# A two-layer hybrid decoder on one core: the list scheduler's durations for the matmul engine are rewritten

## The chip, the cores and the metric

The kernel runs on one NeuronCore of one Trainium2 chip. The metric is the device time of one execution in microseconds (us); lower is better. Shown are the median of three runs, and one execution that the hardware profiler recorded.

## What is computed

Two decoder layers, for a prompt of 512 tokens and for 8 sequences of 8 new tokens (64 more), 576 tokens in all. Each layer projects the normalised input, runs a chunked retention and a sparse attention (an indexer picks the 128 or 66 best keys), gates both, merges them and projects again. All inputs and outputs are fp32. Cut down:

```python
def decoder_layer(x, p_i, pos, ret_s0, past, topk, ...):
    h = rmsnorm(x, g_norm)
    rq, rk, rv, rz, aq, ak, av, az, iq, ik, iw, gr, ga = in_projection(h, w_in, pos, q_gain, k_gain)
    o_r, s_new = retention(rq, rk, rv, ret_s0)
    u_r = (group_norm_heads(o_r) * silu(rz)) @ w_o_ret
    o_a = sparse_attention(aq, pos, k_all, v_all, iq, iw, ik_all, topk)
    u_a = (o_a * silu(az)) @ w_o_att
    m = sigmoid(gr) * u_r + sigmoid(ga) * u_a
    x = x + m @ w_out
    x = x + sigmoid(x @ w_ple_gate) * (p_i @ w_ple_proj)
    return x, ak, av, ik, s_new
```

## The kernel before

**The work.** Every projection is computed in fp32r from two parts: a weight tile of 128x1024 fp32 is loaded by SyncE (SP), rounded by ScalarE (ACT) into `whi`, and the remainder goes to `wlo` by VectorE (DVE) (`convert`, line 440). The moving data are split the same way (`xh`, `xl`). Each block of 128 channels then takes three matmuls: high by high, low by high, high by low. `proj_a` (line 457) makes a 128-channel unit of 48 such matmuls over two halves of 288 tokens, so 288 columns each; the token-major projections take 256, 260 or 320 columns. They write three PSUM banks called `pm`, which DVE and ACT empty.

**The order.** The kernel is written as many sequential generators ("streams"): the main stream, which walks through PLAN (projections, merge, output, gating), and side streams: statistics, tables, the indexer, attention heads (`head`, line 898, three in flight), the sample's attention, retention, and one for each weight load and each bank to be emptied. A stream yields one instruction at a time. `Streams.go` (line 277) is a list scheduler that runs while the program is built: it keeps a clock for each engine, asks for each waiting instruction when its inputs would be ready (`_ready`, line 251), picks the one that could start first (on a tie the lower priority number, then the older stream), emits it, and moves the engine's clock by `op.dur`. On the chip each engine executes its own instructions in the order emitted, and semaphores hold an instruction until its inputs are there. So the durations do not change any instruction; they decide the order on all five queues: PE, DVE, ACT, POOL and SP.

**The table of durations** is `_duration` (line 142). For PE it gives a transpose 0.110 us; a matmul in fp32r `max(n, 64) / 2400 + 0.003` us for n columns; one in plain fp32 `4 * max(n, 64) / 2400` us, times 0.55 when the stationary tile has at most 64 columns, and a small figure when it has at most 32. For DVE it gives (n + 64) / 960 us and for ACT (n + 112) / 1200 us (61 in place of 112 out of PSUM), with additions for scalar pointers. To the end of a producer `_ready` adds a hand-over time (`HOP`, line 199: 0.23 us from ACT to PE, 0.21 from DVE to PE), and for a DVE or ACT instruction fed by another engine a margin of 0.15 or 0.1 us (`MARGIN`, line 103).

**Places that matter below.** An attention head multiplies queries with keys into bank `tq` (two fp32r matmuls), takes the softmax on DVE and ACT (tile `t2k`, row sums in `sm`), transposes the result on PE into bank `ta`, copies it out by ACT, and multiplies with the values into bank `oT`. That last step is in plain fp32 with a stationary tile of 64 columns, one matmul for each block of 128 keys, which the trace shows as two passes. Before the merge the main stream waits for all side streams (line 1254, `for e in sides`), after which the gated results are split into `oh` and `ol`. The only arithmetic on POOL is the power -0.5 in `rsqrt`.

Of the kernel before, what the change touches and what calls it, by code (L numbers as in the profile page):

```python
# [16 lines left out]
OP = mybir.AluOpType  # L17
# [86 lines left out]


class Op:
    __slots__ = ("eng", "fn", "a", "k", "name", "outs", "ins", "dur")

    def __init__(self, eng, fn, name, a, k):
        self.eng, self.fn, self.name, self.a, self.k = eng, fn, name, a, k  # L110
        aps = [x for x in list(a) + list(k.values()) if isinstance(x, bass.AP)]
        out = k.get("out", a[0] if a else None)
        acc = k.get("accum_out")
        self.outs = [_box(x) for x in (out, acc) if x is not None]
        self.ins = [_box(x) for x in aps if x is not out and x is not acc]
        self.dur = _duration(eng, name, out, aps, a, k)


def _val(x):
    return x() if callable(x) else x  # L120


def _box(ap):
    span = 1 + sum(s * (n - 1) for s, n in list(ap.ap)[1:])
    t = ap.tensor
    if ap.space in (bass.MemoryType.SB, PSUM):
        row = list(ap.ap)[0][0] or 1
        p0 = _val(ap.start_partition)
        c0 = ap.offset % row if row > 1 else 0
        return t.name, p0, p0 + _val(ap.partition_size), c0, c0 + span  # L130
    first = list(ap.ap)[0]
    return t.name, 0, 1, ap.offset, ap.offset + span + first[0] * (first[1] - 1)


def _free(ap):
    n = 1
    for s, c in list(ap.ap)[1:]:
        n *= c
    return n


def _duration(eng, name, out, aps, a, k):
    n = max(_free(x) for x in aps)
    psum = any(x.space == PSUM for x in aps[1:])
    if eng == "PE":
        if name == "transpose":
            return 0.110
        lhs = aps[1]
        if lhs.dtype == FT:
            if _free(lhs) <= 32:  # L150
                return 0.030 + n * 0.4e-3
            return 4 * max(n, 64) / 2.4e3 * (0.55 if _free(lhs) <= 64 else 1.0)
        return max(n, 64) / 2.4e3 + 0.003
    if eng == "DVE":
        if name == "memset":
            return (n + 8) / 0.96e3
        ptr = sum(1 for x in aps[1:] if _free(x) == 1 and n > 4 and x.space != PSUM)
        if name in ("tensor_scalar", "tensor_copy") and not psum and all(x.dtype == FT for x in aps[:2]):
            return (n / 2 + 66) / 0.96e3 + 0.062 * min(ptr, 2)
        return (n + 64) / 0.96e3 + 0.062 * min(ptr, 2)  # L160
    if eng == "ACT":
        ptr = sum(1 for x in aps[1:] if _free(x) == 1 and n > 1)
        return (n + (61 if psum else 112)) / 1.2e3 + 0.093 * min(ptr, 2)
    if eng == "POOL":
        return 0.3 + 0.165 * n
    return {"page": 0.5, "gather": 0.74}.get(name, 0.47)


# [24 lines left out]


class Streams:
    """Emits the instructions of many sequential streams in the order in which a model of the engines could
    start them, so that each engine's program order follows what is ready."""

    HOP = {("DVE", "DVE"): 0.13, ("ACT", "ACT"): 0.13, ("POOL", "POOL"): 0.1, ("PE", "PE"): 0.0, ("SP", "SP"): 0.0,
           ("ACT", "PE"): 0.23, ("DVE", "PE"): 0.21, ("PE", "DVE"): 0.2, ("PE", "ACT"): 0.2, ("POOL", "DVE"): 0.07,  # L200
# [2 lines left out]
    def __init__(self):  # L203
        self.clock = dict.fromkeys(("PE", "DVE", "ACT", "POOL", "SP"), 0.0)
        self.dma = 0.0
        self.log = {}
        self.heads = []
        self.run = []
        self.count = 0

    def spawn(self, gen, prio):
        self.count += 1
        self.run.append(([gen, prio, self.count, None, 0.0], None))
# [63 lines left out]
    def go(self):  # L277
        clock = self.clock
        while True:
            while self.run:  # L280
                st, value = self.run.pop(0)
                self._advance(st, value)
            if not self.heads:
                return
            best = None
            for i, st in enumerate(self.heads):
                key = (max(clock[st[3].eng], st[4]), st[1], st[2])
                if best is None or key < best[0]:
                    best = (key, i)
            st = self.heads.pop(best[1])  # L290
            op = st[3]
            start = best[0][0]
            op.fn(*op.a, **op.k)  # L293
            end = start + op.dur
            clock[op.eng] = end
            if op.eng == "SP" and op.name != "page":
                size = _val((op.a[0] if op.a else op.k["out"]).nbytes)
                self.dma = max(self.dma, start + 1.1) + size / 0.35e6
                end = self.dma + 1.0
            self._note(op, end)  # L300
            self._advance(st, None)
# [3 lines left out]
def tile_hybrid_decoder(ctx: ExitStack, tc: tile.TileContext, A, O):  # L305
# [3 lines left out]
    V, S, PE, SP, G = (Engine(n, o) for n, o in (("DVE", nc.vector), ("ACT", nc.scalar), ("PE", nc.tensor),  # L309
                                                 ("SP", nc.sync), ("POOL", nc.gpsimd)))  # L310
# [78 lines left out]
    ready, paged = Event(), Event()  # L389
    second, third = Event(), Event()  # L390

    # ---- weights: one ordered sequence of units, each split into two float32r parts as it lands
    W = {}

    class Unit:
# [1155 lines left out]
```

## Time and profile before

| | |
|---|---|
| three runs | 1131.04, 1131.97, 1132.43 us; median 1131.97 |
| span of the profiled execution | 1130.3 us, 21562 instructions (its own time is not given apart from the span) |
| PE (matmuls) | 1116.5 us busy, 99%, 8586 instructions |
| weight loads of PE | 1058.9 us, 94% |
| DVE / ACT / POOL | 725.6 / 512.5 / 45.7 us busy (64%, 45%, 4%) |
| DMA | 105.92 MB, mean 94 GB/s |

Matmuls overlap in the records: a matmul of 288 columns is shown as 0.30 us long, but the next one starts 0.13 us after it. What PE spends on an instruction is therefore read from start to start in the timeline, not from the duration of one.

### The profile page before, as it was taken

What the parts mean: (1) busy time and instruction counts of PE and PEld (TensorE: products, weight loads), DVE (VectorE), ACT (ScalarE), POOL (GpSimd) and SP (SyncE); (2) the same over time, 40 slices, a digit from 0 to 9 for tenths busy, and PEclk for the clock granted to TensorE, in tenths of its full rate; (3) what the DMA queues carried; (4) which work ended last, traced back from release to release, by engine and by line L of the source; (5) the groups of instructions that cost most, each with busy time, mean ns of one, the idle gap of its engine ahead of it and who ended that gap; (6) DMA issues with size and microseconds to landing.
All of it is one profiled execution on the core that took longest, in us unless ns stands there. A gap on an engine that the chain in (4) does not pass through costs nothing.

```text
span 1130.3 us, 21562 instructions
## 1 busy us (share of the span) xinstructions
PE 1116.5 (99%) x8586; PEld 1058.9 (94%) x8586; DVE 725.6 (64%) x1883; ACT 512.5 (45%) x1084; POOL 45.7 (4%) x52
## 2 busy tenths in 40 slices
PE   8999999999999999999999999999999999999998
PEld 7899988888899999999999999888889999999998
DVE  6799988876464444543658999888654553544343
ACT  6643566647443232324546336656563422222331
POOL 0100200000000000000010012000000000000000
PEclk9999999999999999999999999999999999999999
DMA  6442221322122222523336112222212222234231
GB/s 196 139 133 76 76 75 52 102 78 78 59 75 75 93 76 92 172 92 109 100 118 181 59 57 94 74 79 80 73 60 78 75 78 91 75 130 144 93 113 48
DMA packets 43895, 105.92 MB, mean 94 GB/s; under 512 B 6418, under 2 KB 18578, under 8 KB 43794
## 3 DMA queue, kind: packets, MB, share of 16 engines
q1 hardware_dynamic: 43794, 104.55, 27.4%
q8 instruction: 67, 1.10, 0.4%
q14 instruction: 34, 0.28, 0.1%
HBM read 93.61 MB, written 10.91 MB: 92 GB/s over the span
## 4 chain that ended last, share of the span: by engine, by line
PE 91%; DVE 4%; DMA 2%; ACT 2%; issue 1%; SPq 0%; POOL 0%; DVEq 0%; ACTq 0%; POOLq 0%
PE pm L293 72%; PE oT L293 5%; PE tq L293 4%; PE acc L293 3%; PE tr L293 3%; PE ta L293 3%; DVE wlo L293 1%; DMA wst<-in_wb 1%; ACT whi L293 1%; DVE misc L293 1%; DMA x<-in_xT 1%; DVE silz L293 0%; DMA wst<-in_wq 0%; DVE qs L293 0%; DVE ol L293 0%
## 5 line engine op out<-in xcount | busy, mean ns | idle before, releaser
L293 PE MATMUL pm<-xl,whi 128*128 128x288 f32 x1536 | 458.7, 299 | 0.0
L293 PE MATMUL pm<-xh,wlo 128*128 128x288 f32 x1536 | 458.4, 298 | 0.0
L293 PE MATMUL pm<-xh,whi 128*128 128x288 f32 x1536 | 458.0, 298 | 0.4 <-DVE misc L293 0.4
L293 PEld LDWEIGHTS pm<-xl,whi 128*128 128x128 f32 x1536 | 290.1, 189 | 3.2 <-issue 2.4
L293 PEld LDWEIGHTS pm<-xh,whi 128*128 128x128 f32 x1536 | 290.2, 189 | 2.9 <-issue 1.6
L293 PEld LDWEIGHTS pm<-xh,wlo 128*128 128x128 f32 x1536 | 289.9, 189 | 1.8 <-issue 1.4
L293 ACT ACTIVATE whi<-wst 128x1024 fp32r<-128x1024 f32 (+4 forms) x148 | 150.5, 1019 | 280.5 <-PE pm L293 207.7
L293 DVE TENSOR_TENSOR wlo<-wst,whi 128x1024 fp32r<-128x1024 f32 (+4 forms) x148 | 173.0, 1171 | 88.8 <-ACT whi L293 88.5
L293 PE MATMUL pm<-whi,xh 128*128 128x256 f32 (+2 forms) x416 | 117.2, 288 | 0.7 <-ACT xl L293 0.7
L293 PE MATMUL pm<-wlo,xh 128*128 128x256 f32 (+2 forms) x416 | 117.0, 289 | 0.0
L293 PE MATMUL pm<-whi,xl 128*128 128x256 f32 (+2 forms) x320 | 91.0, 284 | 0.0
L293 DVE TENSOR_TENSOR misc<-pm,R 128x288 f32<-128x288 f32 x64 | 29.2, 457 | 90.1 <-PE pm L293 88.7
L293 ACT ACTIVATE t2k<-t2k,sm 128x256 f32<-128x256 f32 (+3 forms) x136 | 75.6, 581 | 22.6 <-DVE sm L293 19.4
L293 PEld LDWEIGHTS pm<-whi,xh 128*128 128x128 f32 x416 | 78.7, 189 | 2.5 <-issue 1.2
L293 PEld LDWEIGHTS pm<-wlo,xh 128*128 128x128 f32 x416 | 78.7, 189 | 1.6 <-issue 1.1
L293 PE MATMUL pm<-oh,whi 128*128 128x288 f32 x240 | 71.0, 296 | 0.0
L293 PE MATMUL pm<-oh,wlo 128*128 128x288 f32 x240 | 70.9, 296 | 0.0
L293 PE MATMUL pm<-ol,whi 128*128 128x288 f32 x240 | 70.9, 295 | 0.0
L293 PEld LDWEIGHTS pm<-whi,xl 128*128 128x128 f32 x320 | 60.5, 189 | 0.1
L293 ACT ACTIVATE misc<-misc 128x288 f32<-128x288 f32 x64 | 27.9, 436 | 60.5 <-DVE misc L293 60.5
L293 DVE MAX8 sm<-xl 128x8 f32<-128x384 f32 (+2 forms) x96 | 52.3, 548 | 0.3
L293 DVE SCALAR_TENSOR_TENSOR misc<-misc,pm 128x288 f32<-128x288 f32 x60 | 26.8, 451 | 39.3 <-PE pm L293 39.3
(231 smaller groups left out, 1654.3 us busy)
## 6 DMA issues: line engine op xcount, KB each, us to landing
wst<-in_wa SPq DMA_DIRECT2D x96, 512.0 KB, 3.5
wst<-in_wb SPq DMA_DIRECT2D x16, 512.0 KB, 4.1
wst<-in_wo SPq DMA_DIRECT2D x16, 512.0 KB, 3.4
s<-in_ckv SPq DMA_DIRECT2D x32, 128.0 KB, 2.4
s<-in_s SPq DMA_DIRECT2D x8, 512.0 KB, 4.3
out_rss<-s SPq DMA_DIRECT2D x8, 512.0 KB, 2.6
x<-in_xT SPq DMA_DIRECT2D x8, 288.0 KB, 4.5
misc<-in_xT SPq DMA_DIRECT2D x8, 288.0 KB, 3.6
```

The lines of the kernel that those rows point to most:

```text
L293: op.fn(*op.a, **op.k)
```

## The change

It edits the scheduler's model of the matmul engine. The entries for fp32r and for plain fp32 matmuls get other formulas; each PE instruction carries its array form (whether the stationary tile has more than 64 rows, and whether it has up to 32, up to 64 or more columns), and when the form differs from that of the PE instruction emitted before, 0.09 us is added to PE's clock after the instruction has been chosen. The POOL entry keeps its figure for powers and gets a smaller one for other operations. Two comments become blank lines. No instruction is added or removed.

```diff
@@ class Op
-    __slots__ = ("eng", "fn", "a", "k", "name", "outs", "ins", "dur")
+    __slots__ = ("eng", "fn", "a", "k", "name", "outs", "ins", "dur", "form")
...
+        self.form = (_val(a[1].partition_size) > 64, min(2, _free(a[1]) - 1 >> 5)) if eng == "PE" else None
@@ def _duration
             if _free(lhs) <= 32:
                 return 0.030 + n * 0.4e-3
-            return 4 * max(n, 64) / 2.4e3 * (0.55 if _free(lhs) <= 64 else 1.0)
-        return max(n, 64) / 2.4e3 + 0.003
+            return 2 * max(0.11, n / 1.2e3 + 0.005)
+        return max(0.108, (n + 32) / 2.4e3)
...
     if eng == "POOL":
-        return 0.3 + 0.165 * n
+        return 0.3 + (0.165 if k.get("op", a[-1]) == OP.pow else 0.0022) * n
@@ class Streams
+        self.form = None
...
             op.fn(*op.a, **op.k)
+            if op.form != self.form and op.eng == "PE":
+                start += 0.09
+                self.form = op.form
             end = start + op.dur
             clock[op.eng] = end
```

## Rows read from the trace of the kernel before

**Rows 1.** The page: engines over the span, the granted clock in 40 slices.
```profile
PE 1116.5 (99%) x8586; PEld 1058.9 (94%) x8586; DVE 725.6 (64%) x1883; ACT 512.5 (45%) x1084; POOL 45.7 (4%) x52
...
PEclk9999999999999999999999999999999999999999
```

**Rows 2.** The chain that ended last, in order of time: start us, us, what.
```profile
315.99 9.71 PE pm L293 x73
326.09 1.42 DVE ol L293 x2
...
332.68 235.60 PE pm L293 x1776
```

**Rows 3.** By stretch: us, PE, PEld, DVE, ACT, POOL busy, PEclk, DMA share, GB/s.
```profile
60.00:140.00 80.00, 79.64 (x613) 75.44 (x612) 75.95 (x232) 34.69 (x76) 9.45 (x9) 1.00 0.26 89
140.00:240.00 100.00, 99.79 (x787) 87.12 (x785) 84.97 (x275) 61.59 (x160) 4.91 (x6) 1.00 0.24 82
```

**Rows 4.** PE's waits over the whole span: us in total, times, longest.
```profile
PE oT L293 <- ACT whi L293: 5.2, 1, 5.2
PE oT L293 <- DVE ol L293: 0.8, 2, 0.4
```

**Rows 5.** Timeline of PE, matmuls of 256 columns, 120.0 to 121.5 us.
```profile
120.02 0.28 PE L293 MATMUL pm<-whi,xl 128*128 128x256 f32 x1
...
121.43 0.28 PE L293 MATMUL pm<-whi,xl 128*128 128x256 f32 x1
```

**Rows 6.** Timeline around a change of array form, 711.2 to 712.1 us.
```profile
711.20 0.29 PE L293 MATMUL pm<-xl,whi 128*128 128x288 f32 x1
...
711.42 0.43 PE L293 MATMUL oT<-t2k,xl 128*64 128x128 f32 x2
...
711.79 0.40 PE L293 MATMUL pm<-xh,wlo 128*128 128x288 f32 x1
...
712.03 0.30 PE L293 MATMUL pm<-xh,whi 128*128 128x288 f32 x1
```

**Rows 7.** Timeline of PE through two attention heads, 285.0 to 288.6 us.
```profile
285.03 1.09 PE L293 MATMUL oT<-t2k,xl 128*64 128x128 f32 x8
286.05 0.66 PE L293 MATMUL ta<-cst,t2k 128*128 128x128 f32 x4
286.46 0.48 PE L293 MATMUL tq<-kdh,qs 128*128 128x512 f32 x1
...
287.01 0.29 PE L293 MATMUL pm<-xl,whi 128*128 128x288 f32 x1
...
288.29 0.54 PE L293 MATMUL oT<-t2k,xl 128*64 128x128 f32 x3
```

**Rows 8.** Groups of PE instructions over the span, shapes kept apart: the product with the values.
```profile
L293 PE MATMUL oT<-t2k,xl 128*64 128x128 f32 x320 | 48.7, 283 | 0.0
```

**Rows 9.** Timeline of all engines around a wait of PE, 49.0 to 49.6 us.
```profile
49.08 0.39 ACT L293 ACTIVATE t2k<-tq 128x256 f32<-128x256 f32 x1
49.53 0.19 PEld L293 LDWEIGHTS tq<-kdh,iqs 128*128 128x128 f32 x1 [0.88 <-ACT t2k L293]
```

**Rows 10.** Timeline of DVE in the crowded stretch, 90 to 96 us.
```profile
90.20 1.22 DVE L293 TENSOR_TENSOR wlo<-wst,whi 128x1024 fp32r<-128x1024 f32 x1
91.34 0.45 DVE L293 SCALAR_TENSOR_TENSOR silz<-tb,silz 128x288 f32<-128x288 f32 x1
91.72 0.07 DVE L293 MATCH_VALUE_LOAD sc<-sm,sc 64x8 f32 x1
```

**Rows 11.** Waits of PE's weight loads in 40 to 326 us: total, times, longest.
```profile
PEld tq L293 <- ACT t2k L293: 0.9, 1, 0.9
PEld ta L293 <- ACT t2k L293: 0.8, 2, 0.4
PEld ta L293 <- DVE misc L293: 0.7, 2, 0.5
PEld ta L293 <- DVE qs L293: 0.5, 2, 0.3
```

## The prediction

> **What bounds the kernel now.** I read the page first. PE is busy for 1116.5 of 1130.3 us and its granted clock is full, 2.4 GHz, in all 40 slices [rows 1]. The chain in order of time comes second: half of each layer is one unbroken run of PE, such as 1776 matmuls in 235.60 us [rows 2]. The views by stretch and of the waits come third: in the attention part DVE is busy for 75.95 of 80 us (95%), later for 85 of 100 [rows 3], and PE hardly waits. Its largest wait, 5.2 us, is for the first weights, and 0.8 us is lost at the two merges [rows 4]. In the first layer's attention part the larger waits of its weight loads come to 2.9 us [rows 11]. So the bound is PE's own work, the same 8586 instructions in any order. An order can change two things only: how often PE waits, and how often it changes its array form.
>
> **What the table says and what the trace says.** Times are from start to start.
> - A matmul of 288 columns took 235.60 / 1776 = 0.1327 us [rows 2]. The old entry is 0.123 (8% short), the new one 0.133.
> - One of 256 columns took (121.43 - 120.02) / 12 = 0.1175 us [rows 5]; old 0.110, new 0.120.
> - The product with the values: 1.02 us for four of them and the change of form behind them, less 0.09 us, makes 0.23 us each [rows 7]; old 4 x 128 / 2400 x 0.55 = 0.117, new 0.223.
> - A change of form: from the last 288-column matmul to the product at 711.42 it is 0.22 us instead of 0.13, so 0.09 us, the new charge. On the way back it costs more: from 711.20 to 712.03 us are 0.83 us, where the three operations alone make 0.133 + 0.223 + 0.133 = 0.49. A round trip costs 0.34 us; the new table charges 0.18 [rows 6].
> - Together, from 285.03 to 288.29 us [rows 7]: four products with the values, four transposes, two matmuls of 512 columns, nine of 288. Measured 3.26 us. Old: 0.47 + 0.44 + 0.43 + 1.11 = 2.45 us. New: 0.89 + 0.44 + 0.45 + 1.20 + 0.18 = 3.17 us. The old model had PE 1.33 times too fast here, the new one is 3% off.
>
> The Trainium skill (TensorE: Matmul & The Clock Gate, "Back-to-back issue gap") speaks against the new entry: N / 2.4 + 2.5 ns, which is 122.5 ns for 288 columns and so the old figure. By it the new table would be 8% too slow for PE, side work would be placed too early in the main stretches, and more waits would follow. The 0.1327 us measured over 1776 matmuls [rows 2] decides for the new figure.
>
> **Part by part.**
>
> *PE's work: 0.* Nothing is added or removed, and the runs after the merges (1776 matmuls, [rows 2]) hold main work only, with nothing to reorder. The end of the span stays. The start is set by the first weights [rows 4], which no table moves.
>
> *POOL's entry: 0.* Every POOL operation is a power, so its figure stays. If one were not, the whole of POOL's 45.7 us [rows 1] is hidden behind DVE's chain work anyway.
>
> *Where side instructions stand.* The scheduler places a transposition, say, where its clock says that the softmax will be done, and fills PE's queue with main matmuls until then. The old clock ran 1.07 (256 columns) to 1.33 times too fast, so the filler lasted longer on the chip than meant, and side instructions found their inputs ready. The new clock is within 3%, so they stand earlier by 7 to 30% of the time that DVE and ACT need. From 49.08 + 0.39 = 49.47 to 49.53 us a hand-over from ACT to PE took 0.06 us [rows 9], where the model counts 0.23; each step into DVE or ACT has a margin of 0.15 or 0.1 us besides. A softmax with four such steps and one hand-over is padded by 2 x 0.15 + 2 x 0.1 + 0.17 = 0.67 us. It needs about 2.5 us, of which 7 to 30% is 0.2 to 0.75. So the padding about covers what the new clock takes away, and most side instructions still arrive after their data. Where queues on ACT or DVE run late, PE waits as it does now, somewhat longer: the six or so larger waits per layer [rows 11] would each grow by 0.1 to 0.3 us, 12 x 0.2 = 2.4 us for both. Some of the present ones fall away as instructions trade places. I take a third of it, **+0.8 us**. Bounds: below, all of the larger waits vanish in both layers (2 x 2.9 = -5.8 us); above, +9 us (the first rival with twice the lag). PE executes in order, so behind a waiting transposition stands the main stream, and behind that the emptying of the `pm` banks by DVE.
>
> *Changes of form: 0.* The charge is added after an instruction has been chosen, so the scheduler does not seek fewer changes; only chance merges two bursts. The product with the values has 320 passes, 160 matmuls [rows 8], in 64 heads, so some 64 round trips of 0.34 us, 22 us. Two heads share one `ta` bank, so their products rarely meet; three bursts more or fewer are +-1 us.
>
> *The other queues.* Weight loads, their rounding on ACT and remainder on DVE, page gathers on SP and the results' stores are reordered too. DMA is busy for a quarter of the attention part [rows 3], so SP has room. Side streams will end earlier, counted in PE instructions. That is worth nothing: already now 73 main matmuls in a row (9.71 us) stand before the merge [rows 2], so the merge does not wait for them. The splits after it, 0.4 us per layer [rows 4], stay.
>
> **Sum.** 1130.3 + 0.8 = 1131.1 us of span. The median of the runs, 1131.97, is 1.7 us above the span of the profiled execution, so **1132.8 us**. A difference within 0.2% (2.3 us, about what a measurement of this kernel can tell from none) counts as no change.
>
> **Rivals.**
>
> *DVE becomes the bound of the crowded stretch; slower.* In 60 to 140 us DVE has only 4 us left [rows 3]. The old table kept PE 7% behind there, which gave DVE that room. With the new one the scheduler fills DVE to its full time by its own figures, and those are a little short: the remainder of a weight tile takes 91.34 - 90.20 = 1.14 us against 1.133, an operation of 288 columns 91.72 - 91.34 = 0.38 against 0.367 (+3.5%) [rows 10], and ACT's 0.39 us at 49.08 [rows 9] against (256 + 61) / 1200 = 0.26. A lag of 5% over 80 us is 4 us, less about 0.7 us of padding, so 3.3 us per layer, 6.6 for both: **1138.6 us**. Against it: DVE's big operations are nearly right, and its backlog is finite. It decides once DVE is busy for more than 99% of a stretch of some 60 us.
>
> *Fewer waits; faster.* A model that has PE, DVE and ACT in step puts the rounding of weights and the emptying of banks where they are due, and waits such as the 0.88 us behind ACT [rows 9] vanish. If two thirds of 5.8 us go, -4 us: **1128 us**. Against it: PE finds its data late in these places although the old order gave it more time, and an earlier place does not help that.
>
> *The order hardly changes.* The tie rules and the main stream's dominance leave PE's order almost as it was: 1132 us. This is inside the forecast.
>
> **How the numbers follow.** No measurable change, which is the forecast together with the third rival: 0.40, its own range 1129.7 to 1134.2 us. Slower, the DVE lag: 0.33. Faster: 0.27. The range reaches from 1127, most of the faster case down to its full 5 us, to 1141, the slower case with nine us of lag: **1127 to 1141 us**, with about one in ten left out on either side.
>
> **What the profile after would show.** Right: PE's busy time and the 1776-matmul runs as before; side instructions on PE earlier, and a longer unbroken main run before each merge than 9.71 us; PE's waits on `ta` and `tq` of the same few us. The rival on the slow side: DVE near 100% in the stretch from 60 us on, and waits of PE for DVE rising by several us. On the fast side: the waits of [rows 11] gone. The forecast is wrong if the time moves by over 2.3 us; and its mechanism is wrong if the number of changes of form moves by more than a dozen, or if the main run before the merge gets shorter.

## The result and the profile after

The changed kernel takes 1156.14 us (median of four runs, 1155.64 to 1156.57) against 1131.68 us: ratio 1.0216, 95% interval 1.0201 to 1.023. That is 24.5 us slower. The forecast was no measurable change (1132.8 us) and the range ended at 1141. Two parts of the page, engines and the engines of the chain:

```profile
PE 1123.2 (97%) x8586; PEld 1058.8 (92%) x8586; DVE 729.0 (63%) x1883; ACT 516.0 (45%) x1084; POOL 46.2 (4%) x52
...
PE 69%; DVE 21%; ACT 4%; issue 2%; DMA 2%; POOL 1%; SPq 0%; DVEq 0%; ACTq 0%; POOLq 0%
```

The engines of the chain in the kernel before:

```profile
PE 91%; DVE 4%; DMA 2%; ACT 2%; issue 1%; SPq 0%; POOL 0%; DVEq 0%; ACTq 0%; POOLq 0%
```

The engines' instructions are the same in number [rows 1]; the span has grown from 1130.3 to 1154.4 us, and the chain now runs through DVE for 21% of it, before for 4%. PE's waits over the whole span, the view of [rows 4]:

```profile
PE oT L295 <- ACT whi L295: 5.8, 2, 5.6
PE ta L295 <- DVE misc L295: 4.3, 5, 2.0
PE ta L295 <- ACT t2k L295: 2.3, 6, 0.6
PE tr L295 <- ACT xh L295: 2.1, 2, 1.6
PE oT L295 <- ACT t2k L295: 1.7, 4, 0.5
PE ta L295 <- ACT misc L295: 1.6, 1, 1.6
PE tq L295 <- DVE sm L295: 1.5, 4, 0.5
```

The first line is the start, as before. All the others are side instructions that PE reached before DVE or ACT was through. This view counts only time in which the pipeline had run empty. Counted over the trace from start to start (a step beyond the shape's own time, where the semaphore came less than 0.07 us before), PE waited some 9.3 us before and 33.7 us now: +24.4 us, which is the whole loss to about 1 us (how much is a wait hangs on what counts as a shape's own time). Changes of form, counted in the same records, went from 294 to 287, so they cost nothing extra.

By stretch the added waits are 13.6 us in the crowded parts (60 to 180 us: 1.5 to 7.7; 620 to 760 us: 1.5 to 8.9), 9.6 us in the rest of the two attention parts, and 1 us in the first 60 us of the two layers together. Busy time by stretch, columns as in [rows 3]:

```profile
60.00:140.00 80.00, 76.68 (x586) 72.21 (x585) 79.01 (x242) 33.35 (x69) 8.01 (x8) 1.00 0.23 75
140.00:240.00 100.00, 97.19 (x766) 80.78 (x764) 78.49 (x252) 62.99 (x165) 6.22 (x5) 1.00 0.23 76
...
620.00:700.00 80.00, 76.71 (x593) 72.27 (x592) 78.30 (x239) 34.75 (x76) 6.00 (x6) 1.00 0.27 86
700.00:800.00 100.00, 95.98 (x756) 82.14 (x756) 80.36 (x261) 61.26 (x157) 5.73 (x6) 0.98 0.22 70
```

In the first 80 us of the crowd DVE went from 75.95 to 79.01 us busy and PE from 79.64 to 76.68; in the second layer (620 to 700 us) DVE went from 75.76 to 78.30 and PE from 79.79 to 76.71. In finer stretches of the changed kernel:

```profile
60.00:80.00 20.00, 19.33 (x149) 17.23 (x148) 19.83 (x65) 8.65 (x20) 0.00 (x0) 1.00 0.27 86
80.00:100.00 20.00, 19.71 (x144) 19.22 (x144) 19.85 (x52) 7.70 (x14) 0.00 (x0) 1.00 0.31 104
100.00:120.00 20.00, 18.66 (x151) 18.30 (x149) 19.91 (x58) 5.69 (x11) 2.01 (x2) 1.00 0.17 55
120.00:140.00 20.00, 18.97 (x147) 17.46 (x147) 19.42 (x71) 11.31 (x27) 6.00 (x6) 1.00 0.18 54
```

DVE does not pause for 60 us, and most of PE's loss follows behind it. The second layer shows the order of the two more plainly:

```profile
640.00:680.00 40.00, 40.00 (x311) 39.74 (x309) 39.86 (x112) 14.88 (x28) 0.00 (x0) 1.00 0.22 71
680.00:700.00 20.00, 17.25 (x136) 15.93 (x135) 19.57 (x68) 9.43 (x24) 6.00 (x6) 1.00 0.22 72
```

For 40 us DVE is full and PE does not pause; in the next 20 us PE loses 2.75 us. What such a wait looks like is seen at 681.9 us (timeline of the changed kernel, DVE and PE):

```profile
681.43 0.68 DVE L295 MAX8 sm<-xl 128x8 f32<-128x512 f32 x1
...
681.89 0.28 PE L295 MATMUL pm<-wlo,xh 128*128 128x256 f32 x1
682.03 0.40 DVE L295 TENSOR_TENSOR misc<-misc,sm 128x256 f32<-128x256 f32 x1
...
682.36 0.48 DVE L295 SCALAR_TENSOR_TENSOR misc<-pm,rcol,gqk 128x256 f32<-128x256 f32 x1
682.75 0.31 DVE L295 TENSOR_TENSOR misc<-misc,cst 128x64 f32<-128x64 f32 x2
...
683.41 0.55 DVE L295 MAX8 sm<-xl 128x8 f32<-128x384 f32 x1
683.88 0.20 DVE L295 TENSOR_TENSOR misc<-misc 128x64 f32<-128x64 f32 x1
...
684.14 0.44 PE L295 MATMUL ta<-cst,misc 128*128 128x128 f32 x2 [1.97 <-DVE misc L295]
```

The transposition of a query waits 1.97 us for the last addition of its rotary step, on a DVE that works without a break, part of it on the indexer's searches (MAX8). The scheduler had put the transposition where, by its table, DVE would have been through.

The start time that the scheduler gave each instruction can be set beside its start in the trace, since kernel and order are the same. From 620 to 680 us the chip fell behind the scheduler's times by 0.6 us more on PE (from 20.3 to 20.9 us) and by 3.1 us more on DVE (from 20.0 to 23.1). At 680 us DVE was thus 2.2 us later than PE, and the wait at 681.9 us, 2.1 us long, is that difference. In the first layer DVE came up to 1.5 us behind PE between 60 and 140 us; in the kernel before it was never more than 0.5 us in these stretches of either layer.

### The profile page after: what moved, and what is told of

Its sections match the earlier page's. It is cut to its first block, busy times and chain, and to the rows that moved or that the text cites. A ratio compares the mean times of both kernels' runs of the same rounds, so it can differ in the third digit from the quotient of the medians.

```text
span 1154.4 us, 21565 instructions
## 1 busy us (share of the span) xinstructions
PE 1123.2 (97%) x8586; PEld 1058.8 (92%) x8586; DVE 729.0 (63%) x1883; ACT 516.0 (45%) x1084; POOL 46.2 (4%) x52
## 4 chain that ended last, share of the span: by engine, by line
PE 69%; DVE 21%; ACT 4%; issue 2%; DMA 2%; POOL 1%; SPq 0%; DVEq 0%; ACTq 0%; POOLq 0%
PE pm L295 54%; DVE xl L295 5%; PE oT L295 4%; DVE sm L295 4%; PE acc L295 3%; PE tr L295 3%; DVE wlo L295 3%; PE tq L295 2%; DVE misc L295 2%; PE ta L295 2%; ACT tb L295 2%; DVE silz L295 1%; DVE t2k L295 1%; ACT whi L295 1%; DVE qs L295 1%
## 5 line engine op out<-in xcount | busy, mean ns | idle before, releaser
L295 DVE MATCH_REPLACE8 xl<-sm,xl 128x384 f32<-128x384 f32 (+2 forms) x96 | 51.7, 539 | 0.0
```

## The experiments

Each is compared with the kernel before, timed beside it (medians of it 1131.6 to 1132.3 us in the four series). "New" is the changed kernel, "old" the kernel before.

| run | edit | us | ratio, 95% interval |
|---|---|---|---|
| e1 | old + new fp32r entry | 1140.82 | 1.0084 (1.0067 to 1.0101) |
| e2 | new with old fp32r entry | 1138.48 | 1.006 (1.0043 to 1.0077) |
| e3 | new + 0.4 us per hand-over to PE | 1151.02 | 1.0171 (1.0154 to 1.0188) |
| e4 | new, DVE x 1.08, ACT x 1.16 | 1137.86 | 1.0053 (1.0036 to 1.0069) |
| e5 | new, DVE x 1.08 | 1144.62 | 1.0111 (1.0094 to 1.0128) |
| e6 | new, ACT x 1.16 | 1151.11 | 1.0167 (1.015 to 1.0184) |
| e7 | new, PE x 0.87 | 1134.92 | 1.0024 (1.0014 to 1.0034) |
| e8 | new, DVE and ACT x 1.16 | 1137.19 | 1.0055 (1.0036 to 1.0075) |
| e9 | e5 + e3 | 1141.75 | 1.0087 (1.007 to 1.0103) |
| e10 | e4 + e3 | 1144.01 | 1.0111 (1.0094 to 1.0128) |
| e11 | old, PE x 0.93 | 1142.65 | 1.0093 (1.0076 to 1.011) |
| e12 | old, DVE x 1.005 | 1136.24 | 1.0039 (1.0024 to 1.0053) |
| e13 | new, DVE x 1.005 | 1157.41 | 1.0222 (1.0205 to 1.0239) |
| e14 | new, PE x 0.93 | 1135.94 | 1.004 (1.0026 to 1.0054) |
| e15 | old, DVE x 0.93 | 1141.44 | 1.0085 (1.0068 to 1.0102) |
| e16 | new, DVE x 1.04 | 1151.26 | 1.0169 (1.0152 to 1.0186) |

### Which part of the change: e1, e2

```diff
-        return max(n, 64) / 2.4e3 + 0.003
+        return max(0.108, (n + 32) / 2.4e3)
```

e1 has this line alone, e2 everything but this line.

> Only the entry for fp32r matmuls is new (0.133 us for 288 columns); plain fp32 and the change of form stay as before. If the loss comes from PE's clock as a whole no longer running ahead, this entry carries most of it in the stretches of 60 to 140 and 620 to 700 us, where nearly all matmuls are fp32r: PE's waits about half way, 1140 to 1146 us. If the loss came from the form charge or the plain fp32 entry alone, the time stays at 1132 us.

> The complement: the plain fp32 entry and the form charge are new, fp32r as before. Clock as a whole: a loss of 6 to 12 us, nearly all of it after 140 us in each layer, where heads and forms change, and DVE in 60 to 140 us stays at about 95% busy. If the two halves add up, this loss and that of the run before make 24 us together.

Measured: +9.2 and +6.8 us, both inside their ranges, but 16 together and not 24. Both halves cost, and more when joined. The stretch of 60 to 140 us, e1 and then e2:

```profile
60.00:140.00 80.00, 78.17 (x598) 73.90 (x598) 78.41 (x243) 36.01 (x77) 8.02 (x8) 1.00 0.23 74
```

```profile
60.00:140.00 80.00, 79.06 (x604) 74.46 (x603) 77.41 (x240) 34.51 (x75) 8.24 (x9) 1.00 0.26 83
```

The fp32r entry, which rules that stretch, brings DVE to 78.41 us and takes 1.5 us from PE there. With the other half DVE reaches 77.41 us (97%), where e2 expected about 95% (76 us), and PE loses 0.6 us there.

### DVE, ACT, or short chains: e3, e4, e5, e6

```diff
+                        if op.eng == "PE" and e[5] != "PE":
+                            r += 0.4
```

is e3. The others are factors behind the table, here e4:

```diff
-        self.dur = _duration(eng, name, out, aps, a, k)
+        self.dur = _duration(eng, name, out, aps, a, k) * {"DVE": 1.08, "ACT": 1.16}.get(eng, 1.0)
```

> The changed kernel with 0.4 us more in the model for each hand-over from another engine to PE, so that PE's side instructions are placed later by that much. If PE waits because chains of DVE and ACT take some tenths longer than the model says (latency), most waits go: 1136 us or less. If DVE as a whole lags behind in the crowded stretch (throughput), 0.4 us covers a tenth of a lag of 4 us per layer, DVE stays near 99% busy in 60 to 140 us, and the time stays above 1145 us.

> The changed kernel with all DVE durations of the table times 1.08 and all ACT durations times 1.16, about the ratio of busy time in the trace to the sum of the table. If the loss is that only PE's entries were made true while DVE and ACT stayed short, it goes: 1130 to 1136 us, with DVE in 60 to 140 us back at about 95% or below. If it comes from PE's true pace itself (no reserve left for scatter), a good part stays: 1140 us or more.

> The changed kernel with the DVE durations of the table times 1.08 alone. If the loss is DVE falling behind its table in the crowded stretches, most of it goes with this factor alone: 1135 to 1143 us, and DVE is below 98% busy in 60 to 140 us. If ACT's short entries carry the loss, it stays above 1148 us.

> The changed kernel with the ACT durations of the table times 1.16 alone. DVE theory: a gain of at most 6 us, since DVE is still at 98 to 99% in 60 to 140 us: 1150 us or more. ACT theory: 1140 us or less.

The pad gives back 5 us, DVE's factor 11.5, ACT's 5.0, both factors 18.3. e3 and e6 came out as expected of a DVE that lags as a whole (above 1145 and 1150 us); e4 and e5 stayed 1.9 and 1.6 us above the ranges of that theory. The 5 us of e3 and e6 are hardly more than the 4.6 us that a shuffle of ties is worth (e12 below). The first two stretches of the pad (e3), and then of DVE's factor (e5), and the crowd with ACT's factor (e6):

```profile
60.00:140.00 80.00, 77.02 (x596) 72.62 (x595) 78.78 (x246) 33.56 (x71) 7.16 (x7) 1.00 0.20 68
140.00:240.00 100.00, 98.26 (x765) 82.67 (x763) 81.91 (x263) 64.18 (x164) 6.41 (x6) 1.00 0.24 81
```

```profile
60.00:140.00 80.00, 79.70 (x614) 75.57 (x613) 77.54 (x236) 36.12 (x76) 8.17 (x8) 1.00 0.22 69
140.00:240.00 100.00, 99.29 (x786) 82.86 (x784) 83.14 (x274) 62.56 (x164) 6.38 (x6) 1.00 0.24 80
```

```profile
60.00:140.00 80.00, 76.69 (x588) 72.58 (x589) 79.18 (x251) 33.53 (x73) 8.09 (x9) 1.00 0.21 67
```

So there are two places. In the crowd neither the pad nor ACT's factor helps (PE 77.02 and 76.69 of 80 us); with DVE's factor PE is back at 79.70. There DVE as a whole falls behind its table, a lag that grows and that no fixed pad covers: set beside the scheduler's times, DVE still comes 2.1 us behind PE in the first crowd with the pad and with ACT's factor, but no more than 0.3 us with its own. After 140 us the pad seems to help (97.19 to 98.26), which would mean that PE is early for single chains there; one run does not show it. Every edit that lets DVE or ACT take longer in the model gave time back, as the theory of pace has it.

The factors of e4 are a reserve and not a correction. They come from busy time, and a record of DVE or ACT runs on after the next instruction has started. From start to start ACT's table fits (kernel before, three instructions without idle time between them):

```profile
287.74 1.06 ACT L293 ACTIVATE whi<-wst 128x1024 fp32r<-128x1024 f32 x1 [0.40 <-PE pm L293]
288.71 0.43 ACT L293 ACTIVATE tb<-silz 128x288 f32<-128x288 f32 x1
289.04 0.71 ACT L293 ACTIVATE t2k<-t2k,sm 128x512 f32<-128x512 f32 x1
```

That is 0.97 us against 0.947 in the table, and 0.33 against 0.333. Over all instructions of the changed kernel that follow the one before without a pause, DVE needs 2% more than its table says, 3 to 4% in the crowd, and ACT 2.6%.

e4 has two waits of its own, and behind them PE ran at the lower clock (column PEclk, the third from the end), which costs 5 x (0.47 + 0.22) = 3.4 us:

```profile
PE tq L295 <- ACT t2k L295: 1.4, 1, 1.4
PE ta L295 <- ACT misc L295: 1.3, 2, 1.2
```

```profile
55.00:60.00 5.00, 4.77 (x22) 4.35 (x22) 4.00 (x19) 1.22 (x5) 0.00 (x0) 0.53 0.43 114
60.00:65.00 5.00, 5.00 (x38) 4.43 (x38) 4.46 (x9) 3.05 (x5) 0.00 (x0) 0.78 0.14 26
```

### PE's pace alone: e7, e14

```diff
-        self.dur = _duration(eng, name, out, aps, a, k)
+        self.dur = _duration(eng, name, out, aps, a, k) * {"PE": 0.87}.get(eng, 1.0)
...
-                start += 0.09
+                start += 0.09 * 0.87
```

e14 has 0.93 in both places.

> The changed kernel with all its PE entries and the form charge times 0.87, so that the model's PE is again about 1.15 times too fast, but evenly over all kinds of matmul. If what counts is PE's pace against that of the DVE and ACT entries, the loss goes wholly: 1128 to 1134 us. If the shape of the new entries (the form charge, the dear plain fp32 matmul) does the harm, 1140 us or more.

> The changed kernel with PE entries and form charge times 0.93, half way to the factor 0.87 (1134.9 us). Pace: 1142 to 1150 us, with PE waiting less than in the changed kernel in 60 to 140 us. Chance: anything from 1133 to 1156 us, with no relation to DVE's busy share there.

Of 24.5 us they give back 21.2 (e7) and 20.2 (e14). Kept in their new proportions, with the charge for the form, the entries do hardly any harm; what did it is their size beside those of DVE and ACT. e7 stayed 0.9 us above its range. e14 lies below the range of pace and inside the wide one of chance, so the time does not follow PE's factor evenly: most of the loss comes in the last 7% of PE's pace. Its crowd:

```profile
60.00:140.00 80.00, 79.41 (x605) 74.66 (x605) 78.06 (x241) 34.37 (x75) 8.19 (x9) 1.00 0.26 85
```

In e14 PE has 79.41 of 80 us although DVE is 98% busy, and beside the scheduler's times DVE is never more than 0.5 us behind PE there.

### The same mismatch without PE's entries, and the trend: e15, e16

> The kernel before with DVE durations times 0.93; no PE entry touched. Pace: DVE is now some 13% short in the model where PE is 7% short (256 columns), so DVE falls behind in 60 to 140 us, is busy there for 98% or more, and PE waits: 1140 to 1148 us. If the new PE entries do harm by themselves, no loss beyond the chance of 5 us: 1132 to 1137 us.

> The changed kernel with DVE durations times 1.04, half way to 1.08 (1144.6 us). Pace: 1147 to 1153 us and DVE between 97 and 99% busy in 60 to 140 us. Chance: outside 1143 to 1157 us.

e15 is the old kernel with `{"DVE": 0.93}` in the line above, e16 the new one with 1.04. e15 is 9.8 us slower, inside its range, and its crowd shows the same picture with none of the change in it (first fence; DVE comes 1.3 us behind PE there). e16 comes to 1151.26 us, inside its range and between 1156.14 and 1144.62 (second fence):

```profile
60.00:140.00 80.00, 77.88 (x596) 73.56 (x595) 78.86 (x247) 35.05 (x76) 8.03 (x8) 1.00 0.21 69
```

```profile
60.00:140.00 80.00, 79.34 (x610) 74.30 (x608) 78.89 (x248) 35.79 (x78) 8.09 (x8) 1.00 0.23 76
140.00:240.00 100.00, 98.44 (x771) 81.36 (x771) 81.39 (x256) 61.87 (x161) 5.71 (x5) 1.00 0.22 74
```

In e16 DVE is as full as in the changed kernel (78.89 us) and yet PE has 79.34. A full DVE is harmless where the scheduler knows it to be full and places PE's instructions by it. The harm is a DVE that is later than the table. What e16 still loses lies elsewhere: after 140 us (98.44 of 100 us), and in the first 60 us, where PE waited 2.5 us for DVE and then ran at a granted clock of 0.50 (50 to 55 us) and 0.84 (55 to 60 us), some 3.3 us. So e16 is no clean point of a trend in DVE's factor.

### How much is chance: e12, e13

A factor of 1.005 on DVE, on the old table (e12) and on the new one (e13).

> The kernel before with DVE durations times 1.005, a change too small to matter by itself but one that reshuffles ties. It shows how far the time moves by the order's chance alone: within 3 us of 1132 if the differences above are effects, 5 us or more if they are mostly chance.

> The changed kernel with DVE durations times 1.005, which reshuffles ties. If the loss is systematic, it stays: 1150 to 1160 us. If most of it was one unlucky order, the time falls below 1146 us.

The old kernel moves by +4.6 us, which lies between its two expectations and nearer to that of chance; the new one moves by +1.3 us, inside its range. So a shuffle of ties alone can be worth some 5 us (with one shuffle of each kernel its spread is not known), and differences of that size between single runs (e7 or e14 against the kernel before, e4 against e8, e3 or e6 against the changed kernel) say nothing of their edits. The 24.5 us and the steps of 10 to 20 us stand clear of it; the 7 to 10 us of e1, e2 and e15 are only about twice as large.

### More reserve: e8, e9, e10, e11

> The changed kernel with DVE and ACT durations both times 1.16. If a reserve on the two engines is what keeps PE from waiting, this has more of it than DVE times 1.08 (1137.9 us) and lands at 1129 to 1135 us, perhaps below the kernel before. If the rest of that run's loss was chance of the order (a single late chain and the slower clock after it), the time scatters by some us with no trend: 1131 to 1142 us.

> The changed kernel with DVE durations times 1.08 and 0.4 us more for each hand-over to PE. If there are two causes, DVE's lag in the crowded stretches (cured by the factor) and short chains through ACT later (eased by the pad), the two cures add: 1144.6 - 5 = 1139.6 us, with PE at 79.5 of 80 us in 60 to 140 us and fewer waits after 140 us than with the factor alone. If both cures act on one cause, it stays at 1143 to 1146 us.

> DVE times 1.08, ACT times 1.16 and the pad of 0.4 us together. If what is left of the loss in the run with both factors (1137.9 us) is the scatter that a pad covers, 1132 to 1135 us; if it is the order of the first 60 us, where weights and tables are still landing, 1136 to 1139 us.

> The kernel before with all its PE entries times 0.93, so PE's clock in the model runs still further ahead. If a lead of PE keeps reducing its waits (9.3 us in the kernel before), 1127 to 1131 us; if the lead is already enough there, no change, 1131 to 1134 us; if side streams now end too late for the merge, 1136 us or more.

None beats the kernel before. e8 does no better than e4 and stays above the range for a reserve, inside that for chance. e9 lies between its two expectations and within the chance of 5 us of either: inconclusive. In its crowd PE does not get the 79.5 us that were expected, and less than with DVE's factor alone (first fence); 2.4 of the 2.7 us are lost in waits between 135 and 140 us. e10 got worse by 6 us against e4 and lies above both its ranges; its long waits are new ones (second fence), 2.7 us behind DVE's copy into a `t2k` tile among them. e11 shows the far side: with PE still further ahead, side streams can end late. In the second layer PE stands 3.7 us before a transposition of the last retention head, with no main work left ahead of the merge (third and fourth fence, waits and timeline). That is only part of its 11 us: it also waits 2.9 us for ACT in the first crowd, and after each of the two waits the granted clock fell (0.63 and 0.69 in the 5 us from 890 and from 895 us, and the last section), 3.4 us each time.

```profile
60.00:140.00 80.00, 77.34 (x594) 72.83 (x594) 77.50 (x240) 35.22 (x77) 7.01 (x7) 0.99 0.23 74
```

```profile
PE ta L297 <- DVE t2k L297: 2.7, 1, 2.7
PE pm L297 <- DVE xh L297: 1.7, 1, 1.7
```

```profile
PE tr L293 <- ACT xh L293: 3.7, 1, 3.7
PE tq L293 <- ACT t2k L293: 2.9, 1, 2.9
```

```profile
885.97 0.39 PE L293 MATMUL acc<-xh,xl 128*128 128x128 f32 x2
890.04 0.33 PE L293 MATMUL tr<-cst,xh 128*128 128x128 f32 x1 [3.69 <-ACT xh L293]
```

## Why the prediction was wrong

**What held.** PE's work and the long main runs did not move: 1776 matmuls in 235.61 us against 235.60 [rows 2]. The only levers were waits and changes of form, and the changes of form stayed (294 to 287). Side instructions did move forward against their data. The new entry is true for the main matmuls: the same 0.1327 us for one of 288 columns, 0.133 in the table.

**The step that failed** is "where side instructions stand": "the padding about covers what the new clock takes away", taken as +0.8 us with an upper bound of +9. It measured +24.4 us of waits. (The bound was also added up wrongly: the first rival with twice its lag is 2 x (8 - 0.7) = 14.6 us. The result lies beyond that too.) Two things were wrong in it. First, it set the padding of one chain (0.67 us) against the time of that chain alone. In the crowd a chain stands in a queue of DVE work without gaps, where margins for hand-overs count for nothing and the error of the table adds up; e3 shows that 0.4 us more of padding does not help there and e5 that 8% on DVE does. Second, it counted only the six or so waits per layer that already showed [rows 11] as likely to grow. But the old clock's lead had let many more side instructions find their data ready, and these now wait too: some 45 waits were counted before, some 100 after.

**The first rival** named the mechanism, DVE behind its own figures while PE no longer is, at 6.6 us and a chance of 0.33. For its own 80 us per layer it was sized well: 3.3 us expected, and the waits in 60 to 140 and 620 to 700 us, counted from start to start, grew by 3.5 and 3.4 us. It missed that the crowd goes on to about 180 and 760 us, with DVE 94 to 98% busy, which makes 13.6 us in all, and that another 9.6 us would be lost where DVE has room. Its mark, DVE over 99% busy, is not the cause: e16 has nearly the changed kernel's share without the loss (98.6 against 98.8%), and the changed kernel itself has 99.7% from 640 to 680 us, where PE does not pause. DVE later than its table is.

**The second rival** hoped that engines in step lose fewer waits. The new table is what it hoped for, with PE (by the prediction's own sum), DVE and ACT all within 2 to 4% of the trace, and it costs 24.5 us. With a reserve on DVE and ACT as well the time is 1137.9 us: most of the loss gone, but no gain over the old table.

**The rule set against the trace.** N / 2.4 + 2.5 ns, from the Trainium skill (TensorE: Matmul & The Clock Gate, "Back-to-back issue gap"), is 122.5 ns for 288 columns. The section gives it for isolated matmuls and not for a stream of weight loads and matmuls such as this one; 132.7 ns were measured here [rows 2], before and after, so as a duration it stays refuted. That more waits would follow came true for another cause. As an entry for the scheduler a figure near it does better than the true one: e14 has 0.133 x 0.93 = 0.124 us.

**The sign beforehand.** The evidence was in the rows: DVE 95% busy [rows 3] and up to 3.5% short [rows 10], PE now within 3%. Until then PE's clock in the model had run 1.07 to 1.33 times too fast and DVE's only a few per cent, so that on the chip DVE and ACT had more time than the scheduler counted. PE, the one engine that loses by waiting, gave up that lead. ACT's 0.39 us against 0.26 in its table, which the prediction counts with it, is no such sign: 0.39 us is the length of the record, and from ACT's start to PE's are 0.45 us [rows 9], where the model counts 0.26 + 0.23 = 0.49. By a sign that the prediction itself had named its mechanism was wrong: the run of main matmuls before the merge, expected to grow from 73, shrank to 63 in both layers (8.31 us in the first):

```profile
327.78 8.31 PE pm L295 x63
...
344.41 235.61 PE pm L295 x1776
```

**Open:** how the 9.6 us outside the crowd divide between ACT's entries, DVE's, and the order's chance. Counted from start to start, about 11 us of waits stand there in the changed kernel, 8.9 with DVE's factor, 6.6 with ACT's and 4.2 with both, but 13.2 in e13, where only ties were shuffled (and 11.8 in place of some 16 in the crowd). So the runs do not separate them, and the parts of 13.6 and 9.6 us are themselves sure to a few us only.

## What to carry to other kernels

In a list scheduler the engines' clocks matter relative to each other. Making the bottleneck engine's table true was a change of pace: it took away a lead that had covered errors of a few per cent elsewhere, so that PE reached its side work too soon and stood still with the main stream behind it. Keep the bottleneck's entries some per cent short on purpose (e14, e7) or give the other engines a reserve (e4, e8); none of the four beat the old table here. Whether tables that are exact for all engines would do is not shown, as no run has them. Too great a lead can delay side streams past their deadline (e11, one run). And judge such edits beside a nudged copy of each kernel, since here half a per cent on one table moved the time by 4.6 us.

## What was not expected of the hardware

Short waits of PE can be followed by a stretch at the lower clock of 1.2 GHz. In the changed kernel PE waited from 757.87 to 759.74 us, in e11 from 130.56 us on for 3 us. The stretches behind these waits (column PEclk, the third from the end), changed kernel and e11:

```profile
755.00:760.00 5.00, 3.42 (x25) 3.07 (x24) 4.84 (x14) 3.87 (x10) 0.70 (x1) 1.00 0.00 0
760.00:765.00 5.00, 4.98 (x35) 3.79 (x34) 4.11 (x11) 2.28 (x8) 0.00 (x0) 0.66 0.32 105
```

```profile
130.00:135.00 5.00, 2.14 (x13) 1.60 (x12) 4.84 (x12) 3.86 (x9) 0.00 (x0) 0.86 0.42 118
135.00:140.00 5.00, 5.00 (x20) 4.38 (x21) 3.37 (x16) 0.69 (x3) 2.47 (x2) 0.50 0.25 93
```

The first stretch costs 5 x 0.34 = 1.7 us. The second costs 5 x (0.14 + 0.50) = 3.2 us and 0.2 us more in the next 5 us (clock 0.96), so that a wait of 3 us cost about twice its length in all. Stretches at 0.50 also stand inside the kernel in the traces of e3, e4, e7, e9, e10, e13 and e16, for 1.7 to 5.1 us each, so they are part of the times above; they need not come in every execution (e16 took 1150.19 us at a mean clock of 1.000 and 1152.72 us at 0.996). The longest single wait of the changed kernel (2.1 us, at 681.9 us) was not followed by one, so length alone did not decide it. In the kernel before the clock was full throughout [rows 1].
